# Two triangular solves on VectorE, modulation chunks queued behind them, h tiles from two fused operations, and a first feed-forward group of six rows

## The chip, the cores and the metric

The kernel runs on one core of one Trainium2 chip. The metric is device time in microseconds (us) of one execution. Five engines take part: TensorE (PE, its weight loads PEld), VectorE (DVE), ScalarE (ACT), GpSimd (POOL) and SyncE (SP), whose queue issues nearly all DMAs. Every engine works through its own list of instructions in order and waits at semaphores for the others.

## What is computed

One transformer layer for 512 tokens of width 2048, in float32. A modulation vector (six parts of 2048) comes from `c`. The input is normalised and modulated, projected, and goes through sparse attention (8 heads) and an RWKV-7 mixer (16 heads of 64); then the output projection and a gated feed-forward block, each added to the residual.

```
mod = silu(c) @ w_ada + b_ada                    # sh1, sc1, gt1, sh2, sc2, gt2
h = rms_norm(x, norm1_g) * (1 + sc1) + sh1
proj = h @ w_in                                  # attention columns, rwkv columns
att = sparse_attention(...)                      # top 128 of the index scores per query
rwkv: state = state*w + (state @ -kk) (kk*a) + v k;  out = state @ r       # 512 steps
x = x + gt1 * (concat(att, rwkv) @ w_out)
h2 = rms_norm(x, norm2_g) * (1 + sc2) + sh2
x = x + gt2 * ((silu(h2 @ w_ffn_gate) * (h2 @ w_ffn_up)) @ w_ffn_down)
```

## The kernel before

Activations lie transposed, 128 features by 512 tokens to a tile. Each large product is made of three passes in a float32 form of reduced precision (fp32r): weights (`wraw`, loaded by SP) are cast to `whi` by ScalarE, VectorE makes the rest `wlo = wraw - whi`, and likewise `h` is held as `hhi` and `hlo`; TensorE adds hi·hi, hi·lo and lo·hi into `acc`. Four `whi` and four `wlo` buffers stand between VectorE and TensorE, so TensorE can run at most four such weight splits ahead of VectorE.

The order is worked out while the program is built: a job list for TensorE (`run_jobs`), and beside it generators (`streams`), each of which adds its instructions when a planned clock says that their inputs are ready (`until`, `room`, `banks`). On the chip each engine then keeps that order, whatever the real times are.

The stages, by the trace's time: modulation of the first norm and the first projections (0 to 160 us); the other projections, with `prep` for the eight pairs of RWKV heads (160 to 560); the two triangular solves (`solve(0)` for pairs 0 to 3 on GpSimd from 364, `solve(1)` for pairs 4 to 7 on VectorE from 594); `scan` over eight chunks, index scores, top-k (MAX8 and MATCH_REPLACE8 on VectorE) and heads (560 to 1130); output projection (1130 to 1277); second norm and feed-forward block (to the end).

A solve (line 781) is 63 steps of a forward substitution, each one or two pairs of a multiplication into `stmp` and an addition into `X`: 69 pairs. The modulation parts gt1, sh2, sc2 and gt2 are made by `ada_stream` (line 968): 256 chunks `wad` of 256 KB from `w_ada`, each added into an accumulator by one VectorE SCALAR_TENSOR_TENSOR (15 of 16; the first is ScalarE's); a group of 64 ends with a transpose, a reduction (`part`), four small matmuls (`pc`) and an addition on VectorE. gt1 is needed at the first `evac_out`, sh2 and sc2 at `norm2`, gt2 at the first `evac_down`: the jobs of `wdown` may not start before `done["ada"] == 16` (line 1449).

`make_h` (line 585) makes an `h` tile from a normalised row: a product with the row factors (VectorE, or GpSimd where `light` is set: 14 of the 16 tiles of the second norm), `hhi` on ScalarE with scale and shift, then the same scale and shift in place on VectorE, and the difference `hlo`. The in-place step overwrites what ScalarE reads. `h2rhs` (line 1367) makes tiles up to three ahead of the one asked for. The first feed-forward jobs (line 1436) run gate rows 0 and 1 and up rows 0 and 1 (two tiles of 128 columns each) side by side over k, so that each new `h2` tile feeds four rows.

Of the kernel before, what the change touches and what calls it, by code (L numbers as in the profile page):

```python
# [23 lines left out]
PAIRS = 8  # L24
# [24 lines left out]
def layer_kernel(ctx, tc, x, c, positions, w_ada, b_ada, norm1_g, w_in, q_norm_g, k_norm_g,  # L49
# [83 lines left out]
    def now():  # L133
        return clk["pe"]

    SLACK = 0.5
    PACE, PACE2 = 2.4, 3.0

# [445 lines left out]

    def make_h(dst, k, src, rbt, gcol, scol, light=False):
        t = G("hx")
        (P if light else V).tensor_tensor(t, src, rbt, op=OP.mult)
        hi, lo = H("hhi"), H("hlo")
        A.activation(hi, t, AF.Identity, scale=gcol, bias=scol)
        V.tensor_scalar(t, t, gcol, scol, op0=OP.mult, op1=OP.add)  # L590
        V.tensor_tensor(lo, t, hi.bitcast(F32), op=OP.subtract)
        dst[k] = (hi, lo)
        return t
# [187 lines left out]
    def solve(g):  # L781
        while done["prep"] < 4 * g + 4:
            yield
        yield from until(nab)
        E, q = ((P, ("pool", 3.0)), (V, ("dve", 3.0)))[g]
        N0, X = B("N"), B("X")
# [181 lines left out]
    def ada_stream():  # L968
# [15 lines left out]
        for i, (bi, k) in enumerate(chunks):  # L984
            while bi >= 12 and not state["ffn"]:
                yield
            while nl < min(i + 3, 192 if bi < 12 else 256):
                load(nl)
                nl += 1
            t = tiles.pop(i)  # L990
            while now() < last + (PACE if bi < 12 else PACE2):
                yield
            yield from until(t)
            yield from room("dve", 1.5 if done["prep"] == PAIRS and not done["topk"] else 3.5)
            last = now()
            if k == 0:
                A.activation(t, t, AF.Copy, scale=ccol(0))
                acc = t
                continue
            V.scalar_tensor_tensor(acc, t, ccol(k), acc, op0=OP.mult, op1=OP.add)  # L1000
            if k == KD - 1:
                start(ada_sum(acc, *blocks[bi]))
# [306 lines left out]
    def evac_out(m0):  # L1309
        def f(ps, which=(0, 1)):  # L1310
            for i in which:
# [5 lines left out]
                if m == 0:  # L1317
                    ssum["t"] = G("ssum")
                    A.activation(ssum["t"], t, AF.Square)
                else:  # L1320
                    sq = G("sqx")
                    A.activation(sq, t, AF.Square)
                    (P if m < KD - 2 else V).tensor_tensor(ssum["t"], ssum["t"], sq, op=OP.add)
        return f
# [18 lines left out]
    def norm2():  # L1343
# [3 lines left out]
        for t in range(NT):  # L1347
            mm(pst[:, t:t + 1], ssum["t"][:, t * 128:(t + 1) * 128], ones)
        st, rr = SM("st"), SM("rr")
# [10 lines left out]
        att["rb2"] = rb2  # L1360
        state["ffn"] = True

    def h2make(k):
        if k < KD and k not in h2:
            make_h(h2, k, x1[k], att["rb2"], gp2[:, k:k + 1], mod["sh2"][:, k:k + 1], light=k >= 2)

# [55 lines left out]

    gbox, ubox = {}, {}

    def first_ffn(j, box, pool, ks):
        if "ps" not in box:
            box["ps"] = [PG("acc") for _ in range(2)]
        for kk, k in enumerate(ks):
# [7 lines left out]
    for k0 in range(0, KD, 2):  # L1436
        for view, box, ev in ((wgate, gbox, evac_gate), (wup, ubox, evac_up)):
            job(view, k0, 2, 0, 256, (lambda j, box=box, k0=k0: first_ffn(j, box, PG, [k0, k0 + 1])),
                after=(lambda box=box, ev=ev: ev(0)(box["ps"])) if k0 == KD - 2 else None)

    for pi, (f0, f1) in enumerate(PARTS):
        for f in range(f0, f1, 2):
            if f == 0:
                continue
            group_T(wgate, f * 128, TWO, ALLK, 4, lambda k: h2[k], evac_gate(f))
            group_T(wup, f * 128, TWO, ALLK, 4, lambda k: h2[k], evac_up(f))
# [112 lines left out]
```

## Time and profile before

| | |
|---|---|
| median of 3 runs | 2753.78 us (2751.93 to 2757.99) |
| profiled execution | 2751.61 us, span 2749.8 us |
| PE busy | 2662.3 us, 97% of the span |
| DVE busy | 1460.1 us, 53% |
| ACT busy | 808.2 us, 29% |
| POOL busy | 332.3 us, 12% |
| mean granted TensorE clock | 0.985 |
| chain that ended last | PE 87%, DVE 5%, DMA 3%, POOL 2% |

Shares over the span hide the stages: VectorE is busy most of the time up to 1100 us and a third of it after 1500 us. TensorE's idle time in a stretch is the stretch less its busy time; a granted clock below 1.00 means that for a part of the stretch TensorE had the lower of its two levels (1.2 GHz instead of 2.4), so (1 - clock) times the stretch is a measure of what that cost.

### The profile page before, as it was taken

Reading aid. Unit: us, or ns where it says so; the run is one execution under the profiler, and the core shown is the slowest. Engines: PE = TensorE matmul, PEld = TensorE weight load, DVE = VectorE, ACT = ScalarE, POOL = GpSimd, SP = SyncE. Lnnn points to the kernel's source line nnn. Section 1 sums busy time; section 2 is a strip of 40 time slices with the busy share of each in tenths; the row PEclk is TensorE's granted clock in tenths of the full one; section 3 lists DMA queues with packets and bytes.
Section 4 is the critical chain, followed back from the end, with each engine's and each line's share of the span. In section 5 each row is a group of like instructions: output and inputs, shape, how many; then the busy total and the mean of one; then the engine's idle time right before and its main releaser. Section 6 shows DMA issues by size and latency. Waiting matters only on the chain.

```text
span 2749.8 us, 35166 instructions
## 1 busy us (share of the span) xinstructions
PE 2662.3 (97%) x13343; PEld 2105.4 (77%) x13343; DVE 1460.1 (53%) x2414; ACT 808.2 (29%) x1467; POOL 332.3 (12%) x346
## 2 busy tenths in 40 slices
PE   7999988889999899998999999999999999999999
PEld 4477766667777687886788888888888888888887
DVE  3478778879878978435754333323333332333333
ACT  3244422332322234323422222222222222222222
POOL 2001168800021221112100000000000000000000
PEclk8999999999999999999999999999999999999999
DMA  9966777484684343332544233233232333232332
GB/s 325 324 232 209 230 195 214 151 218 138 168 256 152 113 148 101 107 116 88 192 168 165 95 97 99 94 99 100 93 100 92 100 100 96 96 100 92 96 108 95
DMA packets 383194, 396.10 MB, mean 144 GB/s; under 512 B 52442, under 2 KB 332320, under 8 KB 383024
## 3 DMA queue, kind: packets, MB, share of 16 engines
q1 hardware_dynamic: 380784, 387.25, 45.2%
q0 software_dynamic: 2096, 6.34, 0.7%
q8 instruction: 105, 1.72, 0.3%
q14 instruction: 65, 0.53, 0.1%
q10 hardware_dynamic: 144, 0.26, 0.0%
HBM read 358.13 MB, written 35.65 MB: 143 GB/s over the span
## 4 chain that ended last, share of the span: by engine, by line
PE 87%; DVE 5%; DMA 3%; POOL 2%; issue 1%; SPq 1%; ACT 1%; DVEq 0%; POOLq 0%; ACTq 0%
PE acc L127 74%; PE vacc L127 3%; PE p L127 2%; PE po L127 2%; SPq L127 1%; DVE wlo L127 1%; PE adaacc L127 1%; DVE wad L127 1%; DMA wada<-in_w_ada_dram 1%; POOL stmp L127 1%; POOL X L127 1%; PE pl L127 1%; DVE hx L127 1%; PE dot L127 1%; PE pA L127 0%
## 5 line engine op out<-in xcount | busy, mean ns | idle before, releaser
L127 DVE TENSOR_TENSOR wlo<-wraw,whi 128x512 fp32r<-128x512 f32 (+2 forms) x860 | 603.8, 707 | 1038.9 <-ACT whi L127 1032.1
L127 PE MATMUL acc<-hhi,whi 128*128 128x512 f32 (+1 forms) x2256 | 913.1, 405 | 6.3 <-ACT hhi L127 6.3
L127 ACT CAST whi<-wraw 128x512 fp32r<-128x512 f32 (+2 forms) x860 | 518.2, 608 | 1299.4 <-PE acc L127 1213.8
L127 PE MATMUL acc<-hhi,wlo 128*128 128x512 f32 (+1 forms) x2256 | 886.1, 393 | 7.7 <-DVE wlo L127 7.7
L127 PE MATMUL acc<-hlo,whi 128*128 128x512 f32 (+1 forms) x2256 | 886.2, 393 | 5.3 <-DVE hlo L127 5.2
L127 PEld LDWEIGHTS acc<-hhi,whi 128*128 128x128 f32 (+1 forms) x2256 | 425.4, 189 | 129.3 <-issue 32.5
L127 PEld LDWEIGHTS acc<-hhi,wlo 128*128 128x128 f32 (+1 forms) x2256 | 425.7, 189 | 102.5 <-DVE wlo L127 11.0
L127 PEld LDWEIGHTS acc<-hlo,whi 128*128 128x128 f32 (+1 forms) x2256 | 425.9, 189 | 98.1 <-DVE hlo L127 9.5
L127 PE MATMUL acc<-act,whi 128*128 128x512 f32 x1408 | 434.9, 390 | 0.0
L127 PEld LDWEIGHTS acc<-act,whi 128*128 128x128 f32 x1408 | 263.3, 188 | 53.8
L127 PE MATMUL acc<-act,wlo 128*128 128x512 f32 x704 | 274.1, 389 | 0.0
L127 DVE SCALAR_TENSOR_TENSOR wad<-wad,cact 128x512 f32<-128x512 f32 x240 | 199.0, 829 | 7.8 <-DMA wad<-in_w_ada_dram 7.4
L127 PEld LDWEIGHTS acc<-act,wlo 128*128 128x128 f32 x704 | 132.2, 188 | 27.6
L127 PE MATMUL acc<-mhi,whi 128*128 128x512 f32 x256 | 100.6, 393 | 0.0
L127 PE MATMUL acc<-mhi,wlo 128*128 128x512 f32 x256 | 99.7, 390 | 0.0
L127 PE MATMUL acc<-mlo,whi 128*128 128x512 f32 x256 | 99.7, 389 | 0.0
L127 DVE SCALAR_TENSOR_TENSOR x<-acc,gt,x 128x512 f32<-128x512 f32 x80 | 57.3, 751 | 45.4 <-PE acc L127 45.4
L127 POOL TENSOR_TENSOR stmp<-X,N 128x504 f32<-128x504 f32 (+33 forms) x69 | 70.8, 1026 | 44.5 <-DMA N<-nab 37.4
L127 POOL TENSOR_TENSOR X<-X,stmp 128x504 f32<-128x504 f32 (+33 forms) x69 | 72.0, 1043 | 5.4
L127 PEld LDWEIGHTS acc<-mhi,wlo 128*128 128x128 f32 x256 | 48.0, 188 | 10.0
L127 PEld LDWEIGHTS acc<-mlo,whi 128*128 128x128 f32 x256 | 48.1, 188 | 9.9
L127 PEld LDWEIGHTS acc<-mhi,whi 128*128 128x128 f32 x256 | 48.1, 188 | 9.8
(256 smaller groups left out, 2088.2 us busy)
## 6 DMA issues: line engine op xcount, KB each, us to landing
wad<-in_w_ada_dram SPq DMA_DIRECT2D x256, 256.0 KB, 4.1
wraw<-in_w_in_dram SPq DMA_DIRECT2D x107, 512.0 KB, 5.5
wraw<-in_w_ffn_down_dram SPq DMA_DIRECT2D x88, 512.0 KB, 3.5
wraw<-in_w_ffn_gate_dram SPq DMA_DIRECT2D x84, 512.0 KB, 3.5
wraw<-in_w_ffn_up_dram SPq DMA_DIRECT2D x84, 512.0 KB, 3.5
wada<-in_w_ada_dram SPq DMA_DIRECT2D x128, 256.0 KB, 6.7
wraw<-in_w_out_dram SPq DMA_DIRECT2D x32, 512.0 KB, 3.5
pk<-pack SPq DMA_DIRECT2D x16, 768.0 KB, 4.4
```

The lines of the kernel that those rows point to most:

```text
L127: return f(*args, **kw)
```

## The change

Both solves run on VectorE. The chunks of gt1 come at a planned distance of 3.6 us instead of 2.4; those of sh2 and sc2 wait until both solves are done and then come at 1.9 us, but with `room` of 0.7 us while top-k runs; those of gt2 wait until all 16 `h2` tiles are placed, not only until the second norm is. `make_h` is two SCALAR_TENSOR_TENSOR on VectorE, with ScalarE adding only the shift between them, and GpSimd has no part in it. The last square of the second norm goes to TensorE as a second term of the sum over features, not through an addition on VectorE. The first feed-forward jobs take gate rows 2 and 3 too, in two banks of the other PSUM pool: six rows for each `h2` tile.

```
-    PACE, PACE2 = 2.4, 3.0
+    PACE1, PACE, PACE2 = 3.6, 1.9, 3.0
...
-    def make_h(dst, k, src, rbt, gcol, scol, light=False):
+    def make_h(dst, k, src, rbt, gcol, scol):
         t = G("hx")
-        (P if light else V).tensor_tensor(t, src, rbt, op=OP.mult)
+        V.scalar_tensor_tensor(t, src, gcol, rbt, op0=OP.mult, op1=OP.mult)
         hi, lo = H("hhi"), H("hlo")
-        A.activation(hi, t, AF.Identity, scale=gcol, bias=scol)
-        V.tensor_scalar(t, t, gcol, scol, op0=OP.mult, op1=OP.add)
-        V.tensor_tensor(lo, t, hi.bitcast(F32), op=OP.subtract)
+        A.activation(hi, t, AF.Identity, bias=scol)
+        V.scalar_tensor_tensor(lo, t, scol, hi.bitcast(F32), op0=OP.add, op1=OP.subtract)
...
-        E, q = ((P, ("pool", 3.0)), (V, ("dve", 3.0)))[g]
+        E, q = V, ("dve", 3.0)
...
-            while bi >= 12 and not state["ffn"]:
+            while (bi >= 12 and not state["ffn"]) or (4 <= bi < 12 and len(solved) < 2):
                 yield
-            while nl < min(i + 3, 192 if bi < 12 else 256):
+            while nl < min(i + 3, 64 if bi < 4 else 192 if bi < 12 else 256):
...
-            while now() < last + (PACE if bi < 12 else PACE2):
+            while now() < last + (PACE1 if bi < 4 else PACE if bi < 12 else PACE2):
                 yield
             yield from until(t)
-            yield from room("dve", 1.5 if done["prep"] == PAIRS and not done["topk"] else 3.5)
+            yield from room("dve", 0.7 if 4 <= bi and not done["topk"] else 3.5)
...
-                    (P if m < KD - 2 else V).tensor_tensor(ssum["t"], ssum["t"], sq, op=OP.add)
+                    if m == KD - 1:
+                        ssum["last"] = sq
+                    else:
+                        (P if m < KD - 2 else V).tensor_tensor(ssum["t"], ssum["t"], sq, op=OP.add)
...
-            mm(pst[:, t:t + 1], ssum["t"][:, t * 128:(t + 1) * 128], ones)
+            mm(pst[:, t:t + 1], ssum["t"][:, t * 128:(t + 1) * 128], ones, True, False)
+            mm(pst[:, t:t + 1], ssum["last"][:, t * 128:(t + 1) * 128], ones, False, True)
...
-        state["ffn"] = True
...
-            make_h(h2, k, x1[k], att["rb2"], gp2[:, k:k + 1], mod["sh2"][:, k:k + 1], light=k >= 2)
+            make_h(h2, k, x1[k], att["rb2"], gp2[:, k:k + 1], mod["sh2"][:, k:k + 1])
+            state["ffn"] = len(h2) == KD
...
-        for view, box, ev in ((wgate, gbox, evac_gate), (wup, ubox, evac_up)):
+        for view, box, pool, f, ev in ((wgate, gbox, PG, 0, evac_gate), (wup, ubox, PG, 0, evac_up), (wgate, g2box, PS, 2, evac_gate)):
```

How the order moves. First, VectorE's list around `prep` of the fifth pair (L is its scan over tokens, kkn, kf and work are its operands, `wlo` the weight splits, `wad` the modulation chunks). Before:

```order
L127 SCALAR_TENSOR_TENSOR L<-reset,sg 128x512
L127 SCALAR_TENSOR_TENSOR kkn<-k,v_231,prb 128x512
L127 TENSOR_SCALAR kf<-at,v_231,der 128x512
L127 TENSOR_TENSOR kf<-k,kf 128x512
L127 SCALAR_TENSOR_TENSOR work<-kkn,sg 128x8x63
L127 TENSOR_SCALAR work<-kkn 128x8
L127 TENSOR_TENSOR work<-r,sg 128x8x64
L127 SCALAR_TENSOR_TENSOR wad<-wad,cact 128x512
L127 TENSOR_TENSOR wlo<-wraw,whi 128x512
L127 TENSOR_TENSOR at<-at,e_3678 128x512
L127 TENSOR_TENSOR work<-kkn,at 128x8x64
```

Now, on the same engine at the same pair:

```order
L127 TENSOR_TENSOR stmp<-X,N 128x384
L127 TENSOR_TENSOR X<-X,stmp 128x8x48
L127 SCALAR_TENSOR_TENSOR wad<-wad,cact 128x512
L127 TENSOR_TENSOR wlo<-wraw,whi 128x512
L127 SCALAR_TENSOR_TENSOR L<-reset,sg 128x512
L127 TENSOR_TENSOR stmp<-X,N 128x423
L127 TENSOR_TENSOR X<-X,stmp 128x9x47
L127 SCALAR_TENSOR_TENSOR kkn<-k,v_231,prb 128x512
L127 TENSOR_SCALAR kf<-at,v_231,der 128x512
L127 TENSOR_TENSOR kf<-k,kf 128x512
L127 TENSOR_TENSOR wlo<-wraw,whi 128x512
```

The pairs of `stmp` and `X` that stood on GpSimd stand between the operations of `prep`, from the 97th weight split to the 141st; between the 100th and the 150th split there are 15 `wad` where there were 47, and from there to the 236th 43 where there were 63; 51 stand behind the 265th, in the output projection, where there were none.

Second, VectorE's list at the end of the first part of the feed-forward block, where the last `up` rows are evacuated (gate, act) and gt2 is ended (tr, part, gt). Before:

```order
L127 SCALAR_TENSOR_TENSOR wad<-wad,cact 128x512
L127 TENSOR_TENSOR gate<-acc,gate 128x512
L127 TENSOR_TENSOR act<-gate,act 128x512
L127 TENSOR_TENSOR gate<-acc,gate 128x512
L127 TENSOR_TENSOR act<-gate,act 128x512
L127 TENSOR_TENSOR wlo<-wraw,whi 128x512
L127 STREAM_TRANSPOSE tr<-wad 128x512
L127 TENSOR_REDUCE part_378<-tr 128x16
L127 TENSOR_TENSOR wlo<-wraw,whi 128x512 x2
L127 TENSOR_TENSOR gt_375<-pc,v_230 128x16
L127 TENSOR_TENSOR wlo<-wraw,whi 128x512 x13
```

Now:

```order
L127 SCALAR_TENSOR_TENSOR wad<-wad,cact 128x512
L127 TENSOR_TENSOR gate<-acc,gate 128x512
L127 TENSOR_TENSOR act<-gate,act 128x512
L127 TENSOR_TENSOR gate<-acc,gate 128x512
L127 TENSOR_TENSOR act<-gate,act 128x512
L127 SCALAR_TENSOR_TENSOR wad<-wad,cact 128x512 x3
L127 STREAM_TRANSPOSE tr<-wad 128x512
L127 TENSOR_REDUCE part_378<-tr 128x16
L127 TENSOR_TENSOR gt_375<-pc,v_230 128x16
L127 TENSOR_TENSOR wlo<-wraw,whi 128x512 x6
```

The evacuation before was that of the second last group (13 splits and another evacuation follow); now it is that of the last group, with three chunks behind it.

Third, TensorE's list at that place. Before, `pc` stood among the products of the last `up` group:

```order
L127 MATMUL acc<-hhi,whi 128x512
L127 MATMUL acc<-hlo,whi 128x512
L127 MATMUL acc<-hhi,wlo 128x512
L127 MATMUL pc<-part_378,cst 32x16 x4
L127 MATMUL acc<-hhi,whi 128x512
L127 MATMUL acc<-hlo,whi 128x512
```

Now it stands between the last product of that group and the first of `wdown`:

```order
L127 MATMUL acc<-hhi,whi 128x512
L127 MATMUL acc<-hlo,whi 128x512
L127 MATMUL acc<-hhi,wlo 128x512
L127 MATMUL pc<-part_378,cst 32x16 x4
L127 MATMUL acc<-act,whi 128x512 x2
L127 MATMUL acc<-act,wlo 128x512
```

159 products stood between `pc` and the first of `wdown` before, none does now.

## Rows read from the trace of the kernel before

**Rows 1.** Stretches: us, PE, PEld, DVE, ACT, POOL busy, granted clock, DMA share, GB/s.

```profile
360.00:560.00 200.00, 172.88 (x859) 127.74 (x857) 174.25 (x203) 62.04 (x119) 163.50 (x160) 0.94 0.63 182
560.00:605.00 45.00, 38.51 (x200) 24.73 (x200) 31.30 (x64) 14.19 (x30) 1.19 (x2) 0.94 1.03 261
605.00:905.00 300.00, 300.00 (x2036) 229.60 (x2035) 253.23 (x506) 79.16 (x157) 33.42 (x41) 1.00 0.57 169
905.00:980.00 75.00, 63.68 (x330) 46.37 (x329) 69.04 (x151) 18.21 (x39) 18.86 (x18) 0.93 0.43 139
...
1275.00:1335.00 60.00, 47.10 (x176) 35.55 (x175) 50.98 (x73) 24.50 (x47) 21.06 (x15) 0.86 0.33 107
...
1550.00:2600.00 1050.00, 1050.00 (x4634) 869.63 (x4633) 336.54 (x494) 272.60 (x446) 0.00 (x0) 1.00 0.30 97
```

**Rows 2.** Waits of PE, 360 to 560 us: total us, times, longest.

```profile
PE pT L127 <- DVE work L127: 17.5, 4, 5.9
```

**Rows 3.** DVE by form, 200 to 360 us, GpSimd nearly idle: busy, mean ns.

```profile
L127 DVE SCALAR_TENSOR_TENSOR wad<-wad,cact 128x512 f32<-128x512 f32 x49 | 37.5, 765 | 4.9 <-DMA wad<-in_w_ada_dram 4.9
L127 DVE TENSOR_TENSOR wlo<-wraw,whi 128x512 fp32r<-128x512 f32 x48 | 33.6, 701 | 23.5 <-ACT whi L127 23.3
L127 DVE TENSOR_TENSOR pack<-pA,cst 128x512 f32<-128x512 f32 x8 | 5.5, 683 | 0.8 <-PE pB L127 0.8
```

**Rows 4.** DVE by form, 364 to 547 us, while GpSimd solves.

```profile
L127 DVE SCALAR_TENSOR_TENSOR wad<-wad,cact 128x512 f32<-128x512 f32 x40 | 46.2, 1156 | 1.4 <-DMA wad<-in_w_ada_dram 1.3
L127 DVE TENSOR_TENSOR wlo<-wraw,whi 128x512 fp32r<-128x512 f32 x37 | 39.7, 1074 | 18.2 <-ACT whi L127 18.1
...
L127 DVE TENSOR_TENSOR pack<-pA,cst 128x512 f32<-128x512 f32 x6 | 4.1, 678 | 0.0
```

**Rows 5.** Tile work on DVE in those two stretches: us, busy (count), clock, DMA.

```profile
200.00:360.00 160.00, 10.58 (x20) 1.00 0.73 223
364.00:547.00 183.00, 18.56 (x20) 0.93 0.59 179
```

**Rows 6.** Tile wad on DVE in two stretches, columns as before.

```profile
360.00:560.00 200.00, 51.28 (x47) 0.94 0.63 182
560.00:980.00 420.00, 46.47 (x61) 0.98 0.59 173
```

**Rows 7.** Tile stmp, all its instructions, 300 to 1100 us: busy by engine.

```profile
sum 800.00, DVE 70.00 POOL 142.52; mean DVE 1.75 POOL 3.56
```

**Rows 8.** Tile wad, and tile stmp on POOL: ns min/median/max, first and last start.

```profile
L127 DVE SCALAR_TENSOR_TENSOR wad<-wad,cact x240: 719/745/1781, 172.3 to 1516.1; 128x512 f32<-128x512 f32 x120
...
L127 POOL TENSOR_TENSOR stmp<-X,N x69: 290/1070/1847, 364.1 to 545.8; 128x270 f32<-128x270 f32 x3, 128x462 f32<-128x462 f32 x3, 128x62 f32<-128x62 f32 x2, 128x120 f32<-128x120 f32 x2
```

**Rows 9.** Tile hx, the operations that make h: ns min/median/max.

```profile
L127 ACT ACTIVATE hhi<-hx,sh,gp x32: 798/813/817, 30.2 to 1332.9; 128x512 fp32r<-128x512 f32 x32
L127 DVE TENSOR_SCALAR hx<-hx,gp,sh x32: 533/545/1515, 31.0 to 1333.7; 128x512 f32<-128x512 f32 x32
L127 DVE TENSOR_TENSOR hlo<-hx,hhi x32: 691/692/1749, 31.6 to 1334.3; 128x512 fp32r<-128x512 f32 x32
L127 DVE TENSOR_TENSOR hx<-xT,rb x16: 679/682/687, 29.4 to 151.5; 128x512 f32<-128x512 f32 x16
```

**Rows 10.** Waits of PE, 0 to 160 us.

```profile
PE acc L127 <- DVE hlo L127: 3.8, 5, 0.8
```

**Rows 11.** Waits of PE at the second norm, 1275 to 1335 us.

```profile
PE acc L127 <- DVE wlo L127: 6.1, 3, 3.1
PE pst L127 <- DVE ssum L127: 2.4, 1, 2.4
```

**Rows 12.** DVE in order of time at the first part's end: start, duration.

```profile
1521.66 0.70 DVE L127 STREAM_TRANSPOSE tr<-wad 128x512 f32<-128x512 f32 x1
...
1564.98 1.28 DVE L127 TENSOR_TENSOR wlo<-wraw,whi 128x512 fp32r<-128x512 f32 x2
```

**Rows 13.** PE in order of time, the first product of wdown.

```profile
1561.49 0.62 PE L127 MATMUL acc<-act,whi 128*128 128x512 f32 x2
```

More of the change, by code (lines that the diff above doesn't have):

```diff
@@ L1420, in finish @@
                          o.rearrange("p (t m) -> p t m", m=256))
-    gbox, ubox = {}, {}
+    gbox, ubox, g2box = {}, {}, {}
     def first_ffn(j, box, pool, ks):
         if "ps" not in box:
-            box["ps"] = [PG("acc") for _ in range(2)]
+            box["ps"] = [pool("acc") for _ in range(2)]
         for kk, k in enumerate(ks):
@@ L1436, in layer_kernel @@
     for k0 in range(0, KD, 2):
-        for view, box, ev in ((wgate, gbox, evac_gate), (wup, ubox, evac_up)):
-            job(view, k0, 2, 0, 256, (lambda j, box=box, k0=k0: first_ffn(j, box, PG, [k0, k0 + 1])),
-                after=(lambda box=box, ev=ev: ev(0)(box["ps"])) if k0 == KD - 2 else None)
+        for view, box, pool, f, ev in ((wgate, gbox, PG, 0, evac_gate), (wup, ubox, PG, 0, evac_up), (wgate, g2box, PS, 2, evac_gate)):
+            job(view, k0, 2, f * 128, 256, (lambda j, box=box, pool=pool, k0=k0: first_ffn(j, box, pool, [k0, k0 + 1])),
+                after=(lambda box=box, ev=ev, f=f: ev(f)(box["ps"])) if k0 == KD - 2 else None)
     for pi, (f0, f1) in enumerate(PARTS):
@@ L1444, in layer_kernel @@
                 continue
-            group_T(wgate, f * 128, TWO, ALLK, 4, lambda k: h2[k], evac_gate(f))
+            if f > 2:
+                group_T(wgate, f * 128, TWO, ALLK, 4, lambda k: h2[k], evac_gate(f))
             group_T(wup, f * 128, TWO, ALLK, 4, lambda k: h2[k], evac_up(f))
```

## The prediction, made before the changed kernel ran

> **What bounds the kernel now.** I read the page's busy shares first: TensorE 97%. What it can lose is its idle time (2749.8 - 2662.3 = 87.5 us) and the time at the lower clock (0.015 of the span, 41 us); the rest is products that the change keeps (13343 of them, and four tiny ones more). So the question is which of these some 128 us go. The stretches [rows 1] say where they lie. From 360 to 560 TensorE idles 27.1 us and the clock of 0.94 costs 12.0; from 560 to 605, 6.5 and 2.7; from 605 to 905 nothing at all; from 905 to 980, 11.3 and 5.3; from 1275 to 1335, 12.9 and 8.4. The rest lies in the first 160 us and at the very end, and the change hardly touches it.
>
> Next the waits in the first of these stretches: TensorE waits for VectorE's `work` four times, 17.5 us and up to 5.9 at a time [rows 2]. VectorE is busy 174 of 200 us there, which looks full. But the same operations are shorter in the stretch before: `wad` 765 ns against 1156, `wlo` 701 against 1074, while `pack`, one of whose inputs lies in PSUM, keeps its 683 and 678 [rows 3, 4]. GpSimd is busy 163.5 us of the slow stretch [rows 1]. So part of VectorE's load there is waiting for GpSimd.
>
> The Trainium skill, SBUF — State Buffer, section "Who interferes with whom", says that a VectorE instruction with two SBUF inputs contends with a GpSimd instruction that reads SBUF, and that whoever starts first keeps the shared ports for its whole instruction. By that rule the slowing goes when GpSimd's solve goes. The trace agrees: the longest `wad` is 1781 ns, 1036 over the median of 745, and the median `stmp` on GpSimd takes 1070 [rows 8].
>
> **The change part by part.** The profiled execution took 2751.6 us; the median of the runs is 2753.8, 2.2 more. I sum against 2751.6.
>
> *Solves and chunks, 360 to 980 us.* VectorE's load there is 174.3 + 31.3 + 253.2 + 69.0 = 527.8 us [rows 1]. Removed: 32 chunks in the slow stretch at 51.28/47 = 1.09 us and 20 after it at 46.47/61 = 0.76 (counts from the order in the section on the change) [rows 6], 35 + 15 = 50 us. Removed too: the slowing of what stays, 37 `wlo` x 0.373 = 13.8, the 20 `work` operations 18.56 - 10.58 = 8.0, 15 `wad` x 0.391 = 5.9, and some 5 for the other operations of `prep` (an estimate from the same ratio), 32 us [rows 3 to 5]. Added: `solve(0)`, which I price as VectorE's own `solve(1)`, the same 69 pairs, 70.0 us against 142.5 on GpSimd [rows 7]. New load 527.8 - 50 - 32 + 70 = 516 us. TensorE's own need in these 620 us is what is left without its losses: 620 - 64.9 = 555. So VectorE would have to be busy 93% if TensorE were to lose nothing. It lost nothing at 253.2/300 = 84%, and 16.6 of 75 us at 92% [rows 1]. Between these I take 86%, the nearer to the stretch without loss since the changed stretch has the same kind of order, a solve between other work: 516/0.863 = 598, **a gain of 22 us**. The bounds: all 65 lost microseconds come back, or VectorE must be busy as long as now and nothing does (a loss is a rival below). Three of the 22 are in 560 to 605, where no `wad` loads compete with the scan's loads; little is in 905 to 980, where the order has 9 chunks instead of 11.
>
> *`make_h`, first norm.* A tile took 682 + 545 + 692 ns on VectorE with a wait for ScalarE between, since the second step overwrites what ScalarE reads [rows 9]; now it takes twice about 745, the price of `wad`, the same operation [rows 8]. `hlo` comes some 0.5 us earlier. TensorE waited 3.8 us for it [rows 10]; the modulation's loads fill the DMA there, so I take **1.5 us**, between 0 and 3.8. The Trainium skill, VectorE: DVE Perf Modes, section "The perf-mode tier table", speaks against the fusion: the step that goes is of the kind that may run at two elements per cycle, those that come are not. The trace shows 545 against 692, not a half [rows 9]; by the page's factor the saving per tile would shrink by 0.2 us and the sum would be the same within 1 us.
>
> *Second norm and first feed-forward rows.* The last addition of squares (0.69 us) leaves TensorE's wait of 2.4 us [rows 11]; four more small products come, so 0.5 is left. Then TensorE waits 6.1 us for `wlo` [rows 11]. VectorE's two steps of a tile take 545 + 692 = 1237 ns where GpSimd is quiet [rows 9]; GpSimd made the first product, and slowed them. The new price is 1.49 us, all on VectorE, and no `wad` stands between. But each pair of tiles now feeds 36 products, not 24, at 0.227 us (1050 us for 4634 in the steady part [rows 1]): 8.2 us, for VectorE's 3.0 + six `wlo` of half width at some 0.4 (an estimate from 701 ns for the whole width [rows 3]) + two waits of 0.81 for ScalarE's `hhi` [rows 9], 7.0 in all. So TensorE bounds this stage, barely. The wait of 3.1 us at its head stays in part, since six operations of three tiles stand before the weights of the third job. I take 21.3 lost now, 16 then, **a gain of 5 us**, between 0 and 13.
>
> *gt2, a new wait.* Its chunks start when all 16 tiles are placed, about 50 us later, and still come at 3.0 us planned. In the new order `pc` stands between the last `up` product and the first of `wdown`, and VectorE has three chunks, a transpose and a reduction behind the last evacuation. Before, the first `wdown` product began at 1561.49, right behind the last `up` product, and VectorE's evacuation ended at 1564.98 [rows 12, 13]. Now TensorE stands until 1564.98 + 3 x 0.745 for the chunks [rows 8] + 0.70 for the transpose [rows 12] and about as much for the reduction = 1568.6: some 7 us idle. Everything behind waits with it, for the products of `wdown` are in line behind `pc`. From 360 to 560, where TensorE stood up to 5.9 us at a time, 27.1 us of idle time went with 12.0 of clock [rows 1, 2]; the same ratio makes 3.1, and I take 3.5 for the single longer one. **A loss of 10.5 us**, between 3 (if the planner's distance leaves the chunks early on the chip) and 14.
>
> *Chunks in heads and output projection.* 51 come between the 265th and 318th split, 0.75 us each, under TensorE's products (38 us of VectorE in a stage of some 145): what hides them is ample but for the last two heads, where chunks stand in VectorE's chain from logits to `mixed`, and two transposes stand before their `po` without products between. **A loss of 3 us**, between 0 and 8.
>
> Sum: -22 - 1.5 - 5 + 10.5 + 3 = -15: 2736.6, and with the 2.2 us of the median **2739 us**.
>
> **The rivals.** (a) *All is hidden.* The planned clock prices VectorE rightly when GpSimd is quiet, so every wait of 360 to 980 goes: -65, and 8 at the second norm; with 1.5, +10.5 and 0, 2751.6 - 64 + 2.2 = 2690. For it: 605 to 905 loses nothing with a solve on VectorE. Against: the share of 93%.
>
> (b) *VectorE carries TensorE along.* If 84% is all it reaches, as from 605 to 905, 516/0.844 = 611, a gain of 9; with 1.5 + 5 - 13.5 that is -2: 2752, no change. For it: in 360 to 980 TensorE's products are often in line behind one of VectorE's results. Against: TensorE, not VectorE, was full from 605 to 905.
>
> (c) *Slower: the solve fills VectorE.* If the long operations of 360 to 560 do not come from GpSimd, they stay long: 516 + 32 = 548 us, at 86% 635, a loss of 15 in place of the gain: 2751.6 + 15 - 6.5 + 13.5 + 2.2 = 2776. It decides from the point where VectorE needs more than 535 us, that is if more than half of the slowing stays. For it: TensorE waits for VectorE there already. Against: `pack` keeps its time.
>
> **How the numbers follow.** My forecast 0.52, (a) 0.17, (b) 0.18, (c) 0.13. The forecast's own range, from its terms' bounds taken together, is 2712 to 2756. For eight in ten I leave out the far ends of (a) and (c): 2705 to 2765. A difference under 0.2% (5.5 us) can't be told from none. Faster: 0.48 of the forecast, all of (a), 0.07 of (b), 0.72. Same: 0.03 + 0.09 = 0.12. Slower: 0.01 + 0.02 + 0.13 = 0.16.
>
> **What would show it.** `wad` and `wlo` near 765 and 701 ns while the first solve runs (else (c)); TensorE's waits for `work` under 6 us and its losses from 360 to 980 near 43; TensorE standing some 7 us before the first `wdown` product, behind `pc`; no wait for `wlo` over 2 us after the second norm's first tiles. The prediction is wrong if TensorE loses 65 us or more in that stretch, in whatever form, or if the wait at gt2 is not there.

## The result, and the profile after

The changed kernel took 2718.0 us, median of 4 runs (2714.2 to 2725.5), beside 2752.9 of before (4 runs): ratio 0.9874, 95% interval 0.9849 to 0.9899. The forecast of 2739 us had the direction; the gain is 34.8 us where it said 14.8. The profiled execution has a span of 2723.7 us and is the longest of the four.

Stretches of the changed kernel (us, PE, PEld, DVE, ACT, POOL busy, granted clock, DMA share, GB/s):

```profile
360.00:560.00 200.00, 192.26 (x996) 146.15 (x995) 182.45 (x336) 70.87 (x134) 21.28 (x22) 0.98 0.63 175
560.00:605.00 45.00, 42.78 (x243) 31.20 (x241) 35.61 (x70) 12.00 (x24) 1.42 (x2) 0.89 0.64 180
605.00:905.00 300.00, 289.95 (x1968) 218.87 (x1969) 249.97 (x519) 77.96 (x157) 40.21 (x49) 0.96 0.50 148
905.00:980.00 75.00, 72.33 (x362) 55.56 (x361) 54.10 (x118) 27.97 (x66) 17.55 (x20) 1.00 0.44 141
860.00:900.00 40.00, 29.95 (x197) 23.26 (x196) 33.70 (x79) 6.99 (x14) 4.68 (x6) 0.70 0.33 106
```

Beside [rows 1]: from 360 to 605 TensorE now loses 10 us of idle time and 9 by the clock, where it lost 34 and 15. But from 605 to 905, where it lost nothing, it now loses 10 and 12, all of it between 860 and 900. The steady part, 1550 to 2600, is the same: 4634 products without a gap.

VectorE by form, 360 to 535 us, while the first solve runs on it (busy, mean ns | idle before):

```profile
L127 DVE TENSOR_TENSOR wlo<-wraw,whi 128x512 fp32r<-128x512 f32 x48 | 32.9, 693 | 7.5 <-ACT whi L127 7.5
L127 DVE SCALAR_TENSOR_TENSOR wad<-wad,cact 128x512 f32<-128x512 f32 x17 | 13.0, 765 | 0.0
L127 DVE TENSOR_TENSOR pack<-pA,cst 128x512 f32<-128x512 f32 x8 | 5.5, 684 | 0.1
```

The long operations of [rows 4] are as short as in [rows 3]. Both solves on VectorE, tile `stmp` (stretch, busy and count, clock, DMA share, GB/s):

```profile
300.00:1100.00 800.00, 139.94 (x276) 0.97 0.56 166
```

That is 139.94 us busy in 276 instructions, 70.0 a solve, as priced from [rows 7].

The new stall, TensorE from 866 to 896 us in order of time (start, duration, idle before and its releaser). `pst` spreads the row sums `sums` of a head's query or key, `p` and `po` are products of the scan, `SSd` is its state, `acc` stands for the large products:

```profile
869.08 0.24 PE L127 MATMUL pst<-sums,cst 128*32 128x4 f32 x8
873.08 0.29 PE L127 MATMUL pst<-sums,cst 128*32 128x4 f32 x8 [3.76 <-DVE sums L127]
876.92 0.66 PE L127 MATMUL p<-SSd,arc 128*64 128x128 f32 x2 [3.55 <-issue]
...
881.47 1.97 PE L127 MATMUL p<-R,tt 64*64 64x64 f32 x16 [0.90 <-DVE R L127]
```

and VectorE at the same place:

```profile
868.24 0.69 DVE L127 TENSOR_REDUCE sums<-tr 128x16 f32<-128x512 f32 x1
...
871.52 0.69 DVE L127 STREAM_TRANSPOSE tr<-sqq 128x512 f32<-128x512 f32 x1
872.25 0.69 DVE L127 TENSOR_REDUCE sums<-tr 128x16 f32<-128x512 f32 x1
...
875.52 0.41 DVE L127 TENSOR_TENSOR S<-p,S 128x256 f32<-128x256 f32 x1
875.96 0.85 DVE L127 TENSOR_TENSOR SSd<-S,e1c 64x256 f32<-64x256 f32 x2
```

VectorE works without a gap through the preparation of two heads (four operations each between the rows shown) before it comes to the scan's `S` and `SSd`. TensorE has no projection product in its order between these steps: from `pst` at 869 to the first `acc` at 891.67 there is only work that hangs on VectorE and, in one place for 0.5 us, on ScalarE. The wait marked issue ends when `SSd` does.

gt2, TensorE and then VectorE:

```profile
1525.34 0.39 PE L127 MATMUL acc<-hhi,wlo 128*128 128x512 f32 x1
1532.98 0.31 PE L127 MATMUL pc<-part,cst 128*32 128x16 f32 x8 [7.25 <-DVE part L127]
1533.22 1.22 PE L127 MATMUL acc<-act,whi 128*128 128x512 f32 x2
```

```profile
1528.43 0.69 DVE L127 TENSOR_TENSOR act<-gate,act 128x512 fp32r<-128x512 f32 x1 [0.69 <-ACT act L127]
1529.04 2.32 DVE L127 SCALAR_TENSOR_TENSOR wad<-wad,cact 128x512 f32<-128x512 f32 x3
1531.40 0.71 DVE L127 STREAM_TRANSPOSE tr<-wad 128x512 f32<-128x512 f32 x1
1532.14 0.69 DVE L127 TENSOR_REDUCE part<-tr 128x16 f32<-128x512 f32 x1
```

This is the wait that the prediction describes, link by link. At the second norm, where [rows 11] had 6.1 us for `wlo`, TensorE (1240 to 1310 us) waits for none; its longest waits are

```profile
PE acc L127 <- ACT whi L127: 2.1, 1, 2.1
PE acc L127 <- ACT hhi L127: 1.6, 1, 1.6
```

So as not to compare stretches of other content, I read when TensorE reaches the same work: `pw` is the first product of `prep`, `pb` its last, `pl` the first of an attention head, `mhi` the first operand of the output projection, `wdown` the second half of the feed-forward block. Start times from TensorE's rows in order of time, us; the runs named e are below:

| | before | after | e1 | e3 | e5 | e6 | e15 |
|---|---|---|---|---|---|---|---|
| first `pw` | 209.6 | 207.6 | 210.2 | 207.9 | 210.9 | 209.1 | 210.5 |
| last `pb`, end of prep | 556.2 | 534.7 | 535.5 | 534.6 | 552.6 | 517.8 | 516.0 |
| first head's `pl` | 963.4 | 917.2 | 914.0 | 912.0 | 941.0 | 926.4 | 905.1 |
| first product of `mhi` | 1089.4 | 1058.6 | 1055.5 | 1053.5 | 1064.5 | 1053.0 | 1028.6 |
| last of output projection | 1276.5 | 1249.2 | 1246.0 | 1244.0 | 1259.7 | 1240.1 | 1223.7 |
| first of `wdown` | 1561.5 | 1533.2 | 1531.3 | 1518.8 | 1545.4 | 1526.3 | 1507.5 |
| span | 2749.8 | 2723.7 | 2719.0 | 2706.7 | 2733.0 | 2714.7 | 2695.2 |

Between `pw` and `mhi` the profiled execution gained 28.9 us, in the output projection it lost 3.5.

### The profile page after: what moved, and what is told of

It reads as the page before. It is cut to its first block, busy times and chain, and to the rows that moved or that the text cites. A ratio compares the mean times of both kernels' runs of the same rounds, so it can differ in the third digit from the quotient of the medians.

```text
span 2723.7 us, 35144 instructions
## 1 busy us (share of the span) xinstructions
PE 2657.4 (98%) x13351; PEld 2107.0 (77%) x13351; DVE 1459.7 (54%) x2541; ACT 807.9 (30%) x1475; POOL 180.2 (7%) x194
## 4 chain that ended last, share of the span: by engine, by line
PE 90%; DVE 4%; DMA 2%; issue 2%; SPq 1%; ACT 1%; POOL 0%; POOLq 0%; DVEq 0%; ACTq 0%
PE acc L127 77%; PE vacc L127 4%; PE po L127 2%; PE p L127 2%; PE adaacc L127 1%; SPq L127 1%; DMA wada<-in_w_ada_dram 1%; DVE wlo L127 1%; PE dot L127 1%; DMA wraw<-in_w_in_dram 1%; PE pl L127 1%; PE pA L127 0%; PE prb L127 0%; PE pgt L127 0%; DMA xtok<-in_x_dram 0%
## 5 line engine op out<-in xcount | busy, mean ns | idle before, releaser
L127 DVE TENSOR_TENSOR wlo<-wraw,whi 128x512 fp32r<-128x512 f32 (+2 forms) x868 | 580.1, 674 | 1015.1 <-ACT whi L127 1010.7
L127 DVE SCALAR_TENSOR_TENSOR wad<-wad,cact 128x512 f32<-128x512 f32 x240 | 185.4, 772 | 0.9
L127 DVE TENSOR_TENSOR X<-X,stmp 128x462 f32<-128x462 f32 (+21 forms) x138 | 70.7, 512 | 4.9
L127 DVE TENSOR_TENSOR stmp<-X,N 128x462 f32<-128x462 f32 (+21 forms) x138 | 70.0, 507 | 3.9 <-DMA N<-nab 2.2
L127 PE MATMUL vacc<-whi,hhi 128*128 128x512 f32 x128 | 55.7, 435 | 0.0
```

What stands on the lines that cost most here:

```text
L127: return f(*args, **kw)
```

## The experiments

Each time is a median of 4 or 5 runs, its ratio taken to the 7 to 9 runs of before on the same chip (medians 2754.1 to 2756.4), with its 95% interval. Runs of different sets are compared by their gains or ratios; the intervals of two of them overlap when they are less than some 6 us apart, and then only the traces can tell them apart.

**e1: solves and chunk timing without the rest** (on before)

```
-        E, q = ((P, ("pool", 3.0)), (V, ("dve", 3.0)))[g]
+        E, q = V, ("dve", 3.0)
+        (PACE1, PACE, the gate behind both solves and room as changed)
```

> The kernel before with two parts of the change alone: both solves on VectorE, and the new chunk distances and gates of gt1, sh2 and sc2; old make_h, four rows in the first feed-forward group, gt2 gated as before. Theory S: the gain of the change is made by the solve leaving GpSimd, in 360 to 605, and part of it is given back in a stall of some 22 us near 860 to 900, where TensorE's order has no projection products between the last steps of the scan. Then this kernel is as fast as the changed one or a little faster (it lacks 1.9 + 7 us of the first and second norm, and the wait of 11 us at gt2): 2712 to 2722, wad 765 and wlo 700 ns while the first solve runs, losses of TensorE in 360 to 605 near 19 us, in 860 to 900 near 20. Rival C: much of the gain is made elsewhere (make_h, six rows): 2735 to 2745.

2720.3 us, 0.9872 (0.9858 to 0.9887), 36 us less than before. Theory S, with the stall near 870 (29.94 of 40 us busy from 860 to 900); its losses from 360 to 605 are 10 us, not 19.

**e2: the first solve back on GpSimd** (on the changed kernel)

```
-        E, q = V, ("dve", 3.0)
+        E, q = ((P, ("pool", 3.0)), (V, ("dve", 3.0)))[g]
```

> The changed kernel with solve(0) put back on GpSimd. Theory S: wad and wlo are long again (near 1156 and 1074 ns) and TensorE loses 30 us or more in 360 to 605, though 32 chunks fewer stand there; the order no longer runs out of projection products before the heads, so the 20 us of 860 to 900 come back: 2725 to 2740. Rival T (the thinner chunks make the gain, the solve's engine matters little): TensorE loses under 15 us in 360 to 605, and the time is 2700 to 2715. Rival D (the slowing is VectorE's own load, not GpSimd): wad stays near 765 ns with the solve on GpSimd.

2730.6 us, 0.9907 (0.9893 to 0.9922). Its VectorE from 364 to 547 us:

```profile
L127 DVE TENSOR_TENSOR wlo<-wraw,whi 128x512 fp32r<-128x512 f32 x41 | 41.3, 1012 | 29.7 <-ACT whi L127 29.7
L127 DVE SCALAR_TENSOR_TENSOR wad<-wad,cact 128x512 f32<-128x512 f32 x17 | 20.5, 1205 | 0.0
...
L127 DVE TENSOR_TENSOR pack<-pA,cst 128x512 f32<-128x512 f32 x7 | 4.8, 680 | 2.3 <-PE pB L127 2.3
```

Theory S holds, T and D fall: the slowing is back with 17 chunks as with 40. But nearly 26 us of gain stay with the solve on GpSimd: the stall of 860 to 900 is gone, and so is the loss of before from 905 to 980. Moving the solve is thus worth 9 to 12 us with all other parts in place (14 us from e5 to e1, with the chunk timing alone). It was not tried without the chunk timing.

The move has a second way to act here. In before, from 360 to 605, TensorE never waits for GpSimd and VectorE 1.7 us in all. In e2 VectorE stands 6.1 us for the solve's `X`, among whose steps GpSimd's part of `prep` is in line, and TensorE 3.6 us for GpSimd's `sq`, one of that part (7.0 and 4.4 in e5).

**e3: gt2 as before** (on the changed kernel)

```
         att["rb2"] = rb2
+        state["ffn"] = True
...
-            state["ffn"] = len(h2) == KD
```

> The changed kernel with the gate of gt2's chunks as before: open at the end of the second norm, not when all 16 tiles are placed. My step at gt2 prices the wait before the first product of wdown at 10.5 us with its clock: 2707 to 2709, and no wait for pc over 2 us. Rival: the chunks beside the tiles of the second norm delay hlo and wlo there, and TensorE stands for them instead: 2714 to 2720 with waits of 5 us or more between 1250 and 1310.

2709.4 us, 0.9831 (0.9816 to 0.9846): 8 to 12 us faster than the changed kernel in its two sets. TensorE goes from the last `up` product to `wdown` without a wait:

```profile
1518.53 0.39 PE L127 MATMUL acc<-hhi,wlo 128*128 128x512 f32 x1
1518.76 0.62 PE L127 MATMUL acc<-act,whi 128*128 128x512 f32 x2
```

This is the fastest of the versions that compute everything.

**e4: more projections ahead** (on the changed kernel)

```
-        return len(qk) <= (6 if len(scanned) == 2 else 4)
+        return len(qk) <= 6
```

> The changed kernel with one number changed: up to six head tiles of q and k may be made ahead while the scan of the second four pairs still runs, not four. The products then stand between the last steps of the scan, where the changed kernel has none, and fewer are left between the steps of top-k after it. Theory S: the stall of 860 to 900 goes and half of it or less comes back later: 2700 to 2712. Rival: the products are only moved, and TensorE stands between pst, pm and prb of the first heads for as long: 2716 to 2722.

2718.4 us, 0.9867 (0.9851 to 0.9884): no gain. The stall goes from 860 to 900 and comes back behind it:

```profile
860.00:900.00 40.00, 38.13 (x242) 29.48 (x241) 32.88 (x70) 12.19 (x23) 8.87 (x9) 0.96 0.27 81
900.00:1130.00 230.00, 218.86 (x1118) 173.59 (x1117) 184.52 (x358) 86.21 (x186) 57.45 (x53) 0.97 0.53 171
```

In the changed kernel the second stretch had 223.81 and a clock of 1.00. The products are for the most part only moved: of 18 us won in the first stretch 12 are lost in the second, and 3 more in the output projection (193.9 us for 190.6).

**e5: the chunk timing alone** (on before: PACE1, PACE, gate and room as changed)

> The kernel before with the new chunk distances and gates of gt1, sh2 and sc2 alone; solve(0) stays on GpSimd. Theory C (from the run with the solve put back): the chunk timing carries most of the gain, since with fewer chunks among the operations of top-k the waits for sums near 957 to 962 go, though wad stays near 1200 ns in 360 to 560: 2728 to 2736 against 2756 of before. Rival S (moving the solve carries it, and the chunks only make room): 2745 to 2753.

2734.2 us, 0.9926 (0.9912 to 0.9940), 22 us less: theory C. The whole wait for `sums` of before is gone. What TensorE still waits for from 900 to 980 is

```profile
PE pst L127 <- ACT sq L127: 0.6, 1, 0.6
```

(it was 9.1 us for `sums`, 1.8 for `sq`), while prep ends only 3.5 us earlier. In before TensorE's order has no large product between the steps of that wait:

```profile
951.93 0.40 PE L127 MATMUL acc<-hhi,wlo 128*128 128x512 f32 x1
957.77 0.29 PE L127 MATMUL pst<-sums,cst 128*32 128x4 f32 x8 [5.44 <-DVE sums L127]
961.68 0.29 PE L127 MATMUL pst<-sums,cst 128*32 128x4 f32 x8 [3.63 <-DVE sums L127]
961.90 0.80 PE L127 MATMUL acc<-hhi,whi 128*128 128x512 f32 x1
```

**e6: the first solve emptied, on GpSimd** (on before; `tiny` is on for g = 0, and the planner still charges the full shapes)

```
+                if tiny["on"]:
+                    args = [a[:, 0:1, 0:1] for a in args]
                 return f(*args, **kw)
```

> The kernel before, where the 138 operations of solve(0) stay in their places on GpSimd but take one element of a row instead of all; the solve's result is left out. The planned order of all engines is that of before. Theory G (GpSimd's concurrent work makes VectorE's operations long, and these make TensorE wait for work): wad and wlo near 765 and 700 ns in 364 to 547, the four waits for work (17.5 us) under 6 us in all, TensorE's losses in 360 to 605 down from 48 us to 10 to 20, and the time 2722 to 2735. Rival Q (the waits come from the order: chunks in line ahead of work): wad is short, but the waits for work stay above 12 us: 2745 to 2756.

2717.4 us, 0.9862 (0.9848 to 0.9876): 38.6 us less, more than theory G said. (Lines are numbered 4 higher.) GpSimd still works 50 us on the emptied solve, where it worked 142. VectorE from 364 to 547, then TensorE's longest wait from 850 to 980:

```profile
L131 DVE SCALAR_TENSOR_TENSOR wad<-wad,cact 128x512 f32<-128x512 f32 x48 | 36.8, 766 | 3.7 <-DMA wad<-in_w_ada_dram 3.6
L131 DVE TENSOR_TENSOR wlo<-wraw,whi 128x512 fp32r<-128x512 f32 x46 | 31.8, 694 | 26.6 <-ACT whi L131 25.5 <-DMA wad<-in_w_ada_dram 1.0
```

```profile
PE pst L131 <- DVE sums L131: 9.1, 2, 5.5
```

In the same order, all four waits for `work` go (rival Q falls) and prep ends 38 us earlier; the loss before the first heads stays as it was. These are two separate losses.

**e7: the first solve emptied, on VectorE** (the same edit on the changed kernel)

> The changed kernel, where the 138 operations of solve(0) stay in their places on VectorE but take one element of a row; the solve's result is left out. VectorE has some 60 us less to do in 360 to 560, in the same planned order. Theory H (after the change VectorE's solve is hidden, and what is lost at 860 to 900 is made by the order, which has no products there): losses in 360 to 605 fall by under 8 us, the stall of 20 us stays, 2708 to 2717. Rival L (VectorE's load carries TensorE along, as my prediction had it): 2690 to 2700.

2710.2 us, 0.9839 (0.9825 to 0.9853): 8 to 11 us less than the changed kernel by the medians, 6 to 10 by the ratios. An emptied pair still takes 0.37 us, so 46 us of VectorE's work were taken away (93.75 us for both solves' `stmp` and `X` as against 139.94), not 60:

```profile
300.00:1100.00 800.00, 93.75 (x276) 0.98 0.57 169
```

The stall near 870 stays. Some four fifths of what was taken away had been hidden: theory H for the most part, though the losses from 360 to 605 fell by 10 to 12 us (idle 3.4 us for 10.0, clock 0.99 for 0.97), where H said under 8.

**e8: chunks of sh2 and sc2 still later** (on e3)

```
-            while (bi >= 12 and not state["ffn"]) or (4 <= bi < 12 and len(solved) < 2):
+            while (bi >= 12 and not state["ffn"]) or (4 <= bi < 12 and len(scanned) < 2):
```

> The changed kernel with gt2 gated as before (as in the run that did this alone, some 11 us faster than the changed one) and the chunks of sh2 and sc2 behind the scan of the second four pairs, not behind the second solve. Theory H: VectorE is quicker through scan and first top-k, the products left over stand where there are none now, and the stall at 860 to 900 shrinks by half or more: 2695 to 2705. Rival: the planner spends the products earlier again and the stall stays, or the later chunks stand in the heads: 2708 to 2715.

2715.7 us, 0.9859 (0.9845 to 0.9873): 6 to 8 us slower than e3, so theory H missed. `pl` comes 22 us earlier than in e3 (889.6), `mhi` only 1.3 (1052.1): TensorE spends the difference among the heads, and the output projection takes 197.6 us, not 190.5.

**e9: the old `make_h`** and **e10: four rows** (each on e3)

```
-    def make_h(dst, k, src, rbt, gcol, scol):
+    def make_h(dst, k, src, rbt, gcol, scol, light=False):
...
```

```
-    for view, box, pool, f, ev in ((wgate, gbox, PG, 0, ...), (wup, ubox, PG, 0, ...), (wgate, g2box, PS, 2, ...)):
+    for view, box, pool, f, ev in ((wgate, gbox, PG, 0, ...), (wup, ubox, PG, 0, ...)):
...
-            if f > 2:
+            if f > 0:
```

> The kernel with gt2 gated as before (some 11 us faster than the changed one), but with the old three-step make_h, the first product of 14 tiles of the second norm on GpSimd. Between the run without and the run with the new make_h, six rows and the shorter sum of squares, first norm, second norm and first feed-forward group took 1.9 + 10.4 us less. Theory M (make_h is most of it: VectorE's chain bounds the stage): 8 to 12 us slower than that kernel, waits for hlo and wlo of 8 us or more between 1245 and 1310. Rival R (six rows hide the chain whatever make_h costs): 2 to 4 us slower.

> The kernel with gt2 gated as before, but with four rows in the first feed-forward group; new make_h. Theory M: 2 to 4 us slower than the same kernel with six rows. Rival R: 8 to 12 us slower, since 24 products at 0.23 us, 5.4 us, do not cover the 7.0 us of VectorE's and ScalarE's chain for two tiles.

e9 2716.5 us, 0.9857 (0.9842 to 0.9872), e10 2712.3 us, 0.9844 (0.9829 to 0.9858): 7 and 3.5 us slower than e3; the first is under theory M's range, the second in it, but within the intervals. Waits at the second norm (1240 to 1330 us), of e9, of e10 and of e3:

```profile
PE acc L127 <- DVE wlo L127: 4.1, 1, 4.1
PE acc L127 <- ACT hhi L127: 1.6, 1, 1.6
PE acc L127 <- DVE hlo L127: 1.4, 2, 0.9
```

```profile
PE acc L127 <- ACT whi L127: 4.8, 5, 1.6
```

```profile
PE acc L127 <- ACT hhi L127: 1.6, 1, 1.6
PE acc L127 <- ACT whi L127: 1.6, 1, 1.6
```

With four rows it is ScalarE's `whi`, not VectorE, that TensorE waits for. In the stage itself, from the last output product to `wdown`, e3 takes 274.8 us, e9 278.8 and e10 280.0, of which TensorE idles 6.2, 9.9 and 9.7 (6.2 to 6.8 in e8, e11, e12 and e16, which leave this stage as in e3). By the traces the rows are thus worth about as much there as `make_h`, which neither theory M nor R says. 2.3 us of e9's 7 lie before the first `pw`.

**e11: gt1's chunks earlier**, **e12: 16 of sh2 too** (on e3)

```
-    PACE1, PACE, PACE2 = 3.6, 1.9, 3.0
+    PACE1, PACE, PACE2 = 2.4, 1.9, 3.0
```

e12 also moves the gate, the loads, the distance and `room` from group 4 to group 5.

> The kernel with gt2 gated as before, and the 64 chunks of gt1 at a planned distance of 2.4 us, as before, in place of 3.6: they end near 330 us and none stands in prep beside the first solve. Theory H (VectorE's solve is hidden, the stall near 870 is the order's): 0 to 3 us faster, the stall near 870 stays. Rival L (VectorE's load in prep carries TensorE along): 5 to 9 us faster, as with the emptied solve.

> The same with 16 chunks of sh2 too ahead of the solves, at 2.4 us. Theory H: VectorE has 12 us less to do behind the second solve, the top-k comes earlier, and the waits for sums shrink: 0 to 6 us faster than the run with gt1 alone. Rival: the planner orders the products otherwise and the stall moves to the heads, as with the later chunks: 0 to 5 us slower.

2713.8 us, 0.9851 (0.9836 to 0.9866), and 2721.9 us, 0.9876 (0.9859 to 0.9892): 5.5 and 12 us slower than e3. Both my expectations missed. Prep ends at 534.0 and 539.1 against 534.6, so emptying it of chunks buys nothing; e11's first `mhi` comes 3.1 later, and e12 waits 10.3 us for `sums` in all (e3 6.6). Why the planner's other order costs this I did not follow.

**e13: room alone**, **e14: distances and gate alone** (on before)

```
-            yield from room("dve", 1.5 if done["prep"] == PAIRS and not done["topk"] else 3.5)
+            yield from room("dve", 0.7 if 4 <= bi and not done["topk"] else 3.5)
```

> The kernel before with the new bounds of room alone (chunks of sh2, sc2 and gt2 wait for 0.7 us of planned VectorE backlog until top-k is done, gt1's for 3.5); distances and gates as before. Theory A (chunks in VectorE's queue ahead of top-k make the waits for sums near 957 to 962): most of the 22 us of the chunk timing, 2734 to 2742. Rival B (the distances and gates make it, by fewer chunks in prep and scan): 2747 to 2756.

> The kernel before with the new distances (3.6 and 1.9 us) and the gate behind both solves, room as before. Theory A: 2747 to 2756, with waits for sums above 5 us between 900 and 980. Rival B: 2732 to 2742, without them.

2735.6 us, 0.9932 (0.9918 to 0.9945), and 2734.5 us, 0.9926 (0.9914 to 0.9939): 19 and 20 us. Either half removes the waits for `sums` from 900 to 980, and e5 with both has hardly more. My either-or was wrong, and so was its premise, that the chunks in VectorE's line make the wait. e13 has more of them at that place than before (VectorE, tile `wad`, before and then e13):

```profile
930.00:965.00 35.00, 5.42 (x7) 0.00 (x0) 0.85 0.45 147
930.00:965.00 35.00, 6.66 (x9) 0.00 (x0) 1.00 0.47 149
```

What differs is TensorE's planned order: in e13 `acc` products stand on both sides of each `pst` there, from 949 to 962.

**e15: chunk timing, and the first solve emptied on GpSimd** (on before)

> The kernel before with the new chunk timing and with solve(0) emptied on GpSimd (one element of each row; the solve's result is left out). If the two gains are independent, 22 and 38.6 us add: 2692 to 2698. If both are paid from the same waits, the time is near that of the emptied solve alone: 2708 to 2717.

2698.4 us, 0.9796 (0.9783 to 0.9809): 55.7 us less, of 21.9 + 38.6 = 60.5. Nearly independent, 0.4 us past the range for it. There is no stall near 870:

```profile
860.00:900.00 40.00, 39.23 (x191) 28.10 (x191) 34.38 (x69) 9.66 (x17) 13.73 (x12) 1.00 0.37 118
900.00:980.00 80.00, 80.00 (x443) 64.94 (x442) 62.63 (x133) 32.87 (x77) 18.48 (x22) 1.00 0.37 119
```

**e16: e3 and e4 together**

> The changed kernel with gt2 gated as before and up to six head tiles made ahead (the two edits that were tried apart, worth 11 and 0 us). They touch different places, so 2704 to 2710; if the later wait at the heads was hidden by nothing but chance, 2712 or more.

2710.9 us (2704.9 to 2720.9), 0.9844 (0.9824 to 0.9865), not faster than e3, and between the two cases of the expectation.

**e17: the changed kernel once more**

> The changed kernel once more. If its profiled execution was an ordinary one, the median is 2718 to 2724 and TensorE again takes 205 us from the end of prep to the last vacc product; if it was a long one, the median is 2712 to 2719 and that stretch takes 200 to 201 us, as in the runs with the same order there.

2718.7 us (2716.3 to 2722.2), 0.9860 (0.9843 to 0.9876), 37.8 us less than before. From the end of prep to the last `vacc` 203.5 us, between the two marks: undecided. Its profiled execution is the longest again, so the traces show 26 and 29 us of gain (spans 2723.7 and 2720.4), 8 to 9 less than the medians. 7.4 and 3.5 us of that are the profiled executions' distance from their medians; the rest is the profiled execution of before, 1.3 and 4.8 us under the medians that these gains are taken to. Where the shorter executions save time no trace shows.

## Why the prediction was right in direction and wrong in size

**The step that failed** is "Solves and chunks, 360 to 980 us", and in it the term 516/0.863 = 598, a gain of 22 us. Up to the first `mhi` it measured 28.9 in the profiled execution, 32.0 in e17, 34.6 in e1. The step treats VectorE as one fluid load, each microsecond of which costs TensorE 1/0.863. The runs price the pieces apart:

- *The slowing by GpSimd.* I took 32 us of VectorE's time, 37 with the factor. Emptying that solve gave 38.6 (e6). Right in mechanism; that the factor fits here is no evidence for it, since it fails for the next two. The Trainium skill, SBUF — State Buffer, section "Who interferes with whom", has a VectorE instruction with two SBUF inputs contend with a GpSimd instruction that reads SBUF, and one with at most one such input, outside the two-port modes, not: e6 and e2 agree, `wad` 766 and 1205 ns, `pack` 682 and 680.
- *The solve on VectorE.* I charged 70 us, 81 with the factor. e7 took 46 us of it away and got 8 to 11 back; with the same chunk timing, e1 stands 20 us behind e15, where the solve is emptied. So the price is 10 to 20 us, the stall near 870 included. Most of it stands where VectorE has time between what TensorE waits for.
- *The 50 us of chunks.* 58 with the factor; the timing alone gave 22 (e5), and not where I looked. I wrote that little is in 905 to 980; that was false. What goes there is a wait for `sums` at a place where TensorE has no products to put between. Either half of the timing removes it (e13, e14), e13 with more chunks at the place than before. VectorE is still busy 65.6 of the 75 us in e5 and 64.8 in e14, where it was 69.0, and TensorE's order has products there now. That the new order does it, and the lighter load little, is argued from this; no run has the one without the other.

Three large terms were wrong by 2, some 60 to 70 and 36 us and partly cancelled; that the sum came within 7 to 13 us is luck. Two smaller slips: with the 86% of its text, in place of 0.863, the step gives 600 and a gain of 20; and the bounds of the terms add up to 2675 and 2776, so that the range of 2712 to 2756 does not follow from them as stated.

**What I did not see at all** is the stall near 870, 10 us idle and 12 by the clock. With both solves on VectorE the planned order uses up the projections before the last steps of the scan. The order showed it before any run: between `pst` and `pm` there stand no `acc`. The section on the change compares the order at three other places. Filling the place moves most of the loss on (e4), and giving VectorE less to do there (e8) shortens the stall and costs more behind it; in e2, e5 and e15, which leave VectorE's place for the solve free in the plan, it is not there. It is the same fault as the wait for `sums` that before had at 952 to 962.

My sign for the step, "losses from 360 to 980 near 43", came out (10 + 9, 22 and 3 make 44) by two errors: prep recovered more, scan lost new time. The sign for `work` came out as meant: TensorE has no such wait from 360 to 605. And of 28.9 us gained up to `mhi` only 22 are idle time and clock (67 before, 44 after between the same works; the clock's part is 20.5 in both). The other 7 are not explained: `pA` and `pB`, whose 256 products overlap in pairs, kept TensorE busy 20.9 us before and 19.1 after, and I did not settle whether the clock share undercounts.

**make_h, first norm**: first `pw` 2.0 us earlier (forecast 1.5). Single traces scatter by 2 us or more, but the means differ by 2.0 too (209.8 in the eight runs with the old form, 207.8 in the eleven with the new). **Heads and output projection**: 3.5 us lost (forecast 3), read in the output projection alone.

**Second norm and first rows**: 5 forecast, 10.4 measured: from the last output product to `wdown` e1 takes 285.2 us and e3 274.8. Without the new `make_h` 4.0 of it go, without the six rows 5.2 (e9, e10); the shorter sum of squares was not tried alone. I said that TensorE bounds the stage "barely" and kept 16 us of loss for waits that did not come. The Trainium skill, VectorE: DVE Perf Modes, section "The perf-mode tier table", gives a float32 TENSOR_SCALAR in SBUF twice the rate of a TENSOR_TENSOR; here the medians are 546 and 693 ns, and e9, with the three-step form, is slower. One reason is not that table's: its 14 first products on GpSimd stretch VectorE's steps. The operations of `make_h` in e9 (ns min/median/max), then in the changed kernel:

```profile
L127 DVE TENSOR_SCALAR hx<-hx,gp,sh x32: 532/546/1517, 31.2 to 1314.6; 128x512 f32<-128x512 f32 x32
L127 DVE TENSOR_TENSOR hlo<-hx,hhi x32: 691/693/1751, 31.8 to 1315.2; 128x512 fp32r<-128x512 f32 x32
...
L127 POOL TENSOR_TENSOR hx<-x,rb x14: 1272/1446/1737, 1258.1 to 1303.8; 128x512 f32<-128x512 f32 x14
```

```profile
L127 DVE SCALAR_TENSOR_TENSOR hlo<-hx,sh,hhi x32: 750/752/754, 31.3 to 1315.7; 128x512 fp32r<-128x512 f32 x32
L127 DVE SCALAR_TENSOR_TENSOR hx<-x,gp,rb x14: 743/746/750, 1261.5 to 1314.2; 128x512 f32<-128x512 f32 x14
```

Two steps of 750 ns that never stretch do better here than three of which two can take 2.5 times as long and more. ScalarE's `hhi` between them fell too, from 813 to 723 ns (medians), without the scale.

**gt2**: 10.5 forecast; 9.3 up to `wdown` and 2.5 behind it, 1.5 of them by the clock, make 11.8 (e3 against the profiled execution). Idle 7.25 us where I said 7. Right in mechanism and size.

**Rivals.** (c) fell with `wad` at 765 ns, (b) with e7: the products hardly follow VectorE's load. (a), all hidden at 2690, lies 28 us under the time, as the forecast lies 21 over it; but e15, with neither slowing nor stall, is at 2698, so most of what (a) hides can be hidden. e15 leaves out the solve's result and lacks both the gain of the two norms and the wait at gt2, 12.4 and 11.8 us, which are alike.

## What to carry to other kernels

Do not price a change of load by a busy share: price each piece at the waits of the engine that bounds the kernel, and give hidden work nearly nothing. Where an order is planned, read it once from end to end for stretches in which the bounding engine has only work that hangs on another engine; such stretches move when anything before them changes. Work that is started later should keep a margin before the place that needs it: gt2's chunks gave back about a fifth of the gain by ending 7 us too late.

## What the runs showed of the hardware

Cutting GpSimd's solve from 142 us to 50 made the kernel 38.6 us faster, as far as the waits show by what it did to VectorE: `wad` 1156 against 766 ns, `wlo` 1074 against 694, in the same order, with 1.7 us in which VectorE waited for GpSimd and none for TensorE. A VectorE instruction on one element of each partition still took 177 to 192 ns on average (e7), so 138 of them take some 25 us, an estimate for a solve of the smallest shapes.
